# The convolutions' place among the projections, and the normalization behind them moved into their tiles

## The chip, the core and the metric

One core of a Trainium2 chip runs the whole program. The metric is the device time of one execution in microseconds (us). The engines are named as in the profile: PE (TensorE, matrix products; PEld is its weight load), DVE (VectorE), ACT (ScalarE), POOL (GpSimd) and SP (SyncE, which here only issues DMAs). Each works through its own queue in order and waits at semaphores.

## What is computed

One layer of a decoder step: 2048 prompt positions and 32 sample positions share all weights. The input is normalized, multiplied by a wide matrix `w_in`, and split into the inputs of three branches, their SiLU gate paths and three merge gates. The branches are a dilated attention (A), a convolution (B) and a cross-attention into a memory (C).

```python
h = _rmsnorm(x, g_pre) @ w_in
qa, ka, va, za, ub, zb, qc, zc, gt = jnp.split(h, SPLITS, axis=-1)
...
glu = ub[..., :EB] * jax.nn.sigmoid(ub[..., EB:])
conv = causal depthwise convolution of glu, width 31, + conv_b
ob = jax.nn.silu(_layernorm(conv, ln_g, ln_b))
...
mix = (gates[..., 0, :] * ((oa * jax.nn.silu(za)) @ w_pa)
       + gates[..., 1, :] * ((ob * jax.nn.silu(zb)) @ w_pb)
       + gates[..., 2, :] * ((oc * jax.nn.silu(zc)) @ w_pc))
y = x + _rmsnorm(mix @ w_out, g_post)
```

The change concerns branch B: `conv` has 768 channels and 2080 positions, and the LayerNorm runs over the 768 channels of each position.

## The kernel before

All data are float32. A product of two matrices is made from three products of split operands (`gemm`, L160 to L168: high by high, high by low, low by high), so a block of 128 columns of `w_in` against a chunk of positions takes 24 matmuls. A weight block is loaded in one DMA and split by POOL into its high part (L55) and its low part (L56).

**Stages.** `phase_a1` keeps the whole normalized input in SBUF and makes the projections that the branches need: q, k, v (six blocks of 128 columns each), qc (four) and u (six, each of two halves: the gate half, evicted by ACT as a tanh, and the value half, which DVE multiplies into the tile G). In the prediction such a block, or half of a u block, is called a column: there are 32 of them. Each runs over six chunks of positions. A k or v column is also transposed and copied out to rows (`rows_out`, L250 to L265), by PE, DVE and DMA. Two columns of q come first; the others follow in the list `order`: a u block, three others, a u block, three others, and so on. Two DMAs that store a part of the input to memory ride behind each of the first 16 entries.

Behind each u block `conv` (L309 to L352) computes the 31-tap convolution of 128 channels on DVE: the first tap L313, 59 multiply-adds L322 over slices of G into the tile acc, a few small ones for the sample part, and a store of acc to the scratch `d_c` (L335). It also copies the last rows into `so` (L338 to L340), transposes them on PE (L343, L345; PSUM tile trc) and stores them (L350, L351).

Then come, as one stretch, the memory branch (`memory`: `memory_kv` and the cross-attention), the sample attention, the prompt attention, and at the end `phase_c` with the output projections. Beside all of them but the last runs `sweep`: the remaining 40 column blocks of `w_in` (the SiLU paths and gates), whose matmuls write the PSUM tile gg, and whose weights are loaded on ACT's queue.

**conv_norm** (L655 to L687) is the LayerNorm with the SiLU behind it, in nine blocks of 256 positions (the last one of 32) by all six groups of channels. For each: load c (768 KB) from `d_c`; sum the six groups on DVE by one strided reduction (L665); sum over partitions on PE by a matmul with ones (L667); subtract the mean (L668); square on ACT (L671); the same two sums of the squares (L673, L675); variance (L677), square root on ACT and a Newton step on DVE (L63 to L68, from the helper `rsqrt`), multiply (L679); gain and bias on POOL, six instructions (L681); tanh on ACT (L684); the SiLU product on DVE (L685); store (L686). It is a generator: `memory_kv` advances it by one block behind each of its eight weight blocks. Its tiles are its own pool `ln` (c three times, the others once or twice), its PSUM tiles str and sco.

**What sets the order.** The program is written with pools of tiles. A scheduler goes through it once, with a simulated timeline, and fixes each engine's queue. Of the instructions that could start, an engine gets the one with the lowest number, and numbers count up in the order of the text. The helper `later` adds a lag to the numbers of what stands in it:

```python
def later(self, lag):
    p = self.tc.cur_priority
    self.tc.cur_priority = p + lag
    yield
    self.tc.cur_priority = p
```

`conv` is called under `self.later(LAG)` with LAG = 900. Pools are opened and closed like blocks; a pool that is opened later may be laid over the bytes of a closed one. `phase_a1` has psg (four PSUM tiles g), pst (three tr and one trc), cnv (two each of G and GS; one each of gate, acc and others), stg, wr and x12 (the input). With `reuse_waits="tile"`, which psg, pst, cnv and nearly all later pools have, an instruction waits by semaphore only for the users of the bytes that its tile takes.

Of the kernel before, what the change touches and what calls it, by code (L numbers as in the profile page):

```python
# [18 lines left out]
T = S + NS  # L19
# [6 lines left out]
LAG = 900  # L26
# [11 lines left out]
class K:  # L38
# [134 lines left out]
    def phase_a1(self, wp, blocks=None):  # L173
        tc, nc, I, O = self.tc, self.nc, self.I, self.O
        with tc.tile_pool(name="x12", side="right", bufs=1) as xpool, \
                tc.tile_pool(name="stg", side="right", bufs=3) as stg, \
                tc.tile_pool(name="sm1", side="right", bufs=2) as small, \
                tc.tile_pool(name="wr", side="right", bufs=2) as self.wr, \
                tc.tile_pool(name="psg", side="right", bufs=4, space=PSUM, reuse_waits="tile") as psg, \
                tc.tile_pool(name="pst", side="right", bufs=3, space=PSUM, reuse_waits="tile") as pst:  # L180
            for th in (1, 2):
                n = THIRDS[th][1]
                self.X[th] = tuple([xpool.tile([128, n], R32, name=f"x{th}{c}{k}") for k in range(8)]
                                   for c in "hl")
# [12 lines left out]

            with tc.tile_pool(name="cnv", side="right", bufs=1, reuse_waits="tile") as cnv:
                ws.append(self.load_w(wp, self.win(CQ + 128), 8, rp=self.wr))
                for cs, js in [(c, j) for c in (CHUNKS[:1], CHUNKS[1:2], CHUNKS[2:3], CHUNKS[3:4], CHUNKS[4:]) for j in range(2)]:  # L200
                    for s, n in cs:
                        self.chunk("q", js, s, n, ws[js], stg, psg, "g", pst)
                order = []
                rest = [("k", j) for j in range(6)] + [("v", j) for j in range(6)] + \
                       [("q", j) for j in range(2, 6)] + [("qc", j) for j in range(4)]
                for j in range(6):
                    order += [("u", j)] + rest[:3]
                    rest = rest[3:]
                order += rest
                for kind, j in order:  # L210
                    if blocks is not None and (kind, j) not in blocks:
                        continue
                    if kind == "u":
                        gs = self.blk_u(j, wp, stg, cnv, psg, pst)
                        with self.later(LAG):
                            self.conv(j, cnv, pst, *gs)
                    else:
                        self.blk_x(kind, j, wp, stg, psg, pst)
                    for th, c, k in out[:2]:
                        nc.sync.dma_start(self.d_x[th][c][k], self.X[th][c][k].bitcast(F32))  # L220
                    del out[:2]
                assert not out
                self.early = {("za", j): self.load_w(wp, self.win(CZA + 128 * j), 8, rp=self.wr) for j in range(EARLY)}
    def blk_x(self, kind, j, wp, stg, psg, pst):
        w = self.load_w(wp, self.win(self.BASE[kind] + j * 128), 8, rp=self.wr)
# [426 lines left out]
            nc.vector.tensor_add(d, f(O), f(tmp))  # L652


    def conv_norm(self, lp, ps):  # L655
        nc = self.nc
        ones = lp.tile([128, 128], F32, name="ones")
        nc.vector.memset(ones, 1.0)
        W = 256
        for s in range(0, T, W):  # L660
            n = min(W, T - s)
            x = lp.tile([128, 6, W], F32, name="c", bufs=3)[:, :, :n]
            nc.sync.dma_start(x, self.d_c[:, :, s:s + n].rearrange("j p n -> p j n"))
            sm = lp.tile([128, W], F32, name="sm", bufs=2)[:, :n]
            nc.vector.tensor_reduce(sm, x.rearrange("p j n -> p n j"), axis=AX.X, op=ALU.add)  # L665
            p = ps.tile([128, 512], F32, name="str")[:, :n]
            nc.tensor.matmul(p, ones, sm, start=True, stop=True)  # L667
            nc.vector.scalar_tensor_tensor(x, p[:, None, :].to_broadcast([128, 6, n]), -1.0 / EB, x,  # L668
                                           op0=ALU.mult, op1=ALU.add)
            sq = lp.tile([128, 6, W], F32, name="sq", bufs=1)[:, :, :n]  # L670
            nc.scalar.activation(sq, x, AF.Square)  # L671
            sm = lp.tile([128, W], F32, name="sm", bufs=2)[:, :n]
            nc.vector.tensor_reduce(sm, sq.rearrange("p j n -> p n j"), axis=AX.X, op=ALU.add)  # L673
            p = ps.tile([128, 512], F32, name="sco")[:, :n]
            nc.tensor.matmul(p, ones, sm, start=True, stop=True)  # L675
            var = lp.tile([128, W], F32, name="var")[:, :n]
            nc.vector.tensor_scalar(var, p, 1.0 / EB, EPS, op0=ALU.mult, op1=ALU.add)  # L677
            rs = self.rsqrt(lp, var, [128, W], "ln", n)
            nc.vector.tensor_tensor(x, x, rs[:, None, :].to_broadcast([128, 6, n]), op=ALU.mult)  # L679
            for j in range(6):  # L680
                nc.gpsimd.tensor_scalar(x[:, j], x[:, j], self.v("ln_g", j), self.v("ln_b", j),  # L681
                                        op0=ALU.mult, op1=ALU.add)
            t = lp.tile([128, 6, W], F32, name="sq", bufs=1)[:, :, :n]
            nc.scalar.activation(t, x, AF.Tanh, scale=0.5)  # L684
            nc.vector.scalar_tensor_tensor(x, t, 1.0, x, op0=ALU.add, op1=ALU.mult)  # L685
            nc.sync.dma_start(self.d_actb[:, :, s:s + n].rearrange("j p n -> p j n"), x)  # L686
            yield  # L687
# [196 lines left out]
    def memory(self):  # L884
        tc = self.tc
        with tc.tile_pool(name="mem", side="right", bufs=1, reuse_waits="tile") as kp, \
                tc.tile_pool(name="ln", side="right", bufs=1, reuse_waits="tile") as lp, \
                tc.tile_pool(name="lnp", side="right", bufs=1, space=PSUM, reuse_waits="tile") as lps:
            ln = self.conv_norm(lp, lps)
            with tc.tile_pool(name="mem1", side="right", bufs=1, reuse_waits="tile") as mp, \  # L890
                    tc.tile_pool(name="mem1p", side="right", bufs=2, space=PSUM, reuse_waits="tile") as ps, \
                    tc.tile_pool(name="memw", side="right", bufs=2, reuse_waits="tile") as wp:
                KT, VV = self.memory_kv(mp, kp, wp, ps, ln)
            for _ in ln:
                pass
            with tc.tile_pool(name="mem2", side="right", bufs=1, reuse_waits="tile") as mp, \
                    tc.tile_pool(name="mem2p", side="right", bufs=2, space=PSUM, reuse_waits="tile") as ps:
                sc = self.sample_cross(mp, lps)
                for _ in self.cross(mp, ps, KT, VV):
                    for _ in range(3):  # L900
                        next(sc, 0)
                for _ in sc:
                    pass

    def memory_kv(self, mp, kp, wp, ps, ln):
# [12 lines left out]
        rs = self.rsqrt(mp, ss, [128, 2], "mr")  # L918
        for x in range(2):
            nc.vector.tensor_scalar(mts[x], mts[x], rs[:, x:x + 1], None, op0=ALU.mult)  # L920
        for k in range(8):
            t = ps.tile([128, 512], F32, name="tr")
            for x in range(2):
# [3 lines left out]
                                           op0=ALU.mult, op1=ALU.subtract)  # L927
        KT, VV = [], []
        for c in range(8):
            h = c % 4  # L930
            w = self.load_w(wp, I["w_mem_kv"][0, :, 128 * c:128 * c + 128], 8)
            p = ps.tile([128, 512], F32, name="kv")
# [8 lines left out]
            t = ps.tile([128, 512], F32, name="tr")  # L941
# [6 lines left out]
            if c >= 4:  # L948
# [359 lines left out]
```

## Time and profile before

| | |
|---|---|
| median of 3 runs | 3149.05 us (3148.02 to 3153.83) |
| the profiled execution | 3154.4 us, span 3152.6 us |
| PE busy | 3000.2 us, 95% |
| DVE busy | 2014.8 us, 64% |
| ACT, POOL busy | 1124.2 us (36%), 1350.4 us (43%) |
| first tap of the first and last convolution | 154.1 us, 754.9 us |
| last matmul of the projections | 868.3 us |
| blocks of the normalization: first and last Square | 881.9 us, 1125.0 us |
| first and last matmul of the sweep | 869.0 us, 2549.7 us |

The median says what the kernel takes; the stretches and durations are of the one profiled execution. A group's row gives what is written and read, the shape, how often it ran, its busy time, the mean duration in ns, and the idle time of its engine just before it with what ended that. A row of one source line gives the shortest, median and longest duration in ns and the start of the first and of the last. A busy PE is only good as a sign that it has work; idle time of PE is what counts.

### The profile page before, as it was taken

What the parts mean: (1) busy time and instruction counts of PE and PEld (TensorE: products, weight loads), DVE (VectorE), ACT (ScalarE), POOL (GpSimd) and SP (SyncE); (2) the same over time, 40 slices, a digit from 0 to 9 for tenths busy, and PEclk for the clock granted to TensorE, in tenths of its full rate; (3) what the DMA queues carried; (4) which work ended last, traced back from release to release, by engine and by line L of the source; (5) the groups of instructions that cost most, each with busy time, mean ns of one, the idle gap of its engine ahead of it and who ended that gap; (6) DMA issues with size and microseconds to landing.
All of it is one profiled execution on the core that took longest, in us unless ns stands there. A gap on an engine that the chain in (4) does not pass through costs nothing.

```text
span 3152.6 us, 55374 instructions
## 1 busy us (share of the span) xinstructions
PE 3000.2 (95%) x20705; PEld 2839.9 (90%) x20705; DVE 2014.8 (64%) x3734; ACT 1124.2 (36%) x2835; POOL 1350.4 (43%) x1048
## 2 busy tenths in 40 slices
PE   7999999999987999999999999989899979999998
PEld 6899999999987999998999999989898967787897
DVE  5297797796677926465546766666656457556563
ACT  5010010010132433243437575656565523222221
POOL 0121221142356537444256565667676433233240
PEclk9899999999999999999999999999999989999999
DMA  7232222211265454477454656576555487657561
GB/s 250 85 103 80 80 60 61 63 62 50 81 182 167 135 153 144 147 219 239 151 139 116 161 123 163 128 185 150 156 143 152 109 279 227 223 168 227 161 197 53
DMA packets 532218, 454.66 MB, mean 144 GB/s; under 512 B 118191, under 2 KB 458581, under 8 KB 531137
## 3 DMA queue, kind: packets, MB, share of 16 engines
q1 hardware_dynamic: 357502, 335.36, 36.2%
q10 hardware_dynamic: 169840, 105.02, 11.7%
q0 software_dynamic: 4608, 10.75, 1.2%
q8 instruction: 164, 2.69, 0.4%
q14 instruction: 104, 0.85, 0.1%
HBM read 332.96 MB, written 118.04 MB: 143 GB/s over the span
## 4 chain that ended last, share of the span: by engine, by line
PE 70%; DMA 12%; DVE 7%; issue 4%; POOL 3%; ACT 2%; SPq 1%; ACTq 0%; DVEq 0%; POOLq 0%
PE g L166 8%; PE g L167 8%; PE g L168 8%; PE gg L166 6%; PE gg L168 6%; PE gg L167 6%; PE pg L168 3%; PE pg L166 3%; PE pg L167 3%; PE pt L571 2%; DMA cb<-d_cf 2%; PE y L1180 2%; PE y L1179 2%; PE y L1178 2%; PE o L598 1%
## 5 line engine op out<-in xcount | busy, mean ns | idle before, releaser
L166 PE MATMUL gg<-x0h,whi 128*128 128x256 f32 (+1 forms) x2560 | 747.9, 292 | 25.9 <-DVE st L246 12.2
L168 PE MATMUL gg<-x0h,wlo 128*128 128x256 f32 (+1 forms) x2560 | 741.8, 290 | 0.1
L167 PE MATMUL gg<-x0l,whi 128*128 128x256 f32 (+1 forms) x2560 | 741.1, 290 | 0.0
L55 POOL TENSOR_SCALAR whi<-wraw 128x1024 fp32r<-128x1024 f32 x162 | 242.7, 1500 | 928.5 <-PE g L167 524.1
L166 PEld LDWEIGHTS gg<-x0h,whi 128*128 128x128 f32 x2560 | 493.2, 193 | 35.0 <-DVE st L246 13.7
L167 PEld LDWEIGHTS gg<-x0l,whi 128*128 128x128 f32 x2560 | 493.5, 193 | 2.2 <-issue 0.5
L168 PEld LDWEIGHTS gg<-x0h,wlo 128*128 128x128 f32 x2560 | 493.2, 193 | 2.2 <-POOL wlo L56 0.3
L322 DVE SCALAR_TENSOR_TENSOR acc<-G,cw,acc 128x1536 f32<-128x1536 f32 (+15 forms) x354 | 480.8, 1408 | 0.3
L56 POOL TENSOR_TENSOR wlo<-wraw,whi 128x1024 fp32r<-128x1024 f32 x162 | 417.0, 2575 | 9.4 <-PE gg L168 0.2
L155 POOL TENSOR_TENSOR clo<-craw,chi 128x768 fp32r<-128x768 f32 (+1 forms) x96 | 174.1, 1815 | 346.0 <-ACT chi L154 329.8
L627 ACT ACTIVATE P<-T,stm 128x128 f32<-128x128 f32 (+1 forms) x576 | 260.8, 455 | 141.0 <-DVE stm L625 94.8
L239 ACT ACTIVATE st<-g 128x384 f32<-128x384 f32 (+1 forms) x132 | 60.2, 461 | 570.7 <-PE g L168 550.7
L166 PE MATMUL pg<-ac,chi 128*128 128x512 f32 (+1 forms) x640 | 229.4, 359 | 16.6 <-ACT chi L154 8.7
L625 DVE CUSTOM_DVE_ANT_0 T<-s,bias 128x128 f32<-128x128 f32 (+1 forms) x576 | 191.5, 357 | 80.8 <-PE s L617 47.0
L167 PE MATMUL pg<-ac,chi 128*128 128x512 f32 (+1 forms) x640 | 228.8, 358 | 6.3 <-DVE ac L1198 6.3
L168 PE MATMUL pg<-ac,clo 128*128 128x512 f32 (+1 forms) x640 | 227.6, 357 | 3.6 <-POOL clo L155 3.6
L576 DVE TENSOR_TENSOR pl<-pt,ph 128x512 fp32r<-128x512 f32 x240 | 155.6, 652 | 52.4 <-ACT ph L575 48.9
L168 PE MATMUL g<-x0h,wlo 128*128 128x384 f32 x544 | 184.3, 339 | 2.9 <-POOL wlo L56 2.9
L166 PE MATMUL g<-x0h,whi 128*128 128x384 f32 x544 | 183.6, 338 | 2.6 <-ACT st L239 2.3
L167 PE MATMUL g<-x1l,whi 128*128 128x384 f32 x544 | 186.0, 342 | 0.0
L167 PE MATMUL g<-x0l,whi 128*128 128x384 f32 x544 | 185.8, 342 | 0.0
L168 PE MATMUL g<-x1h,wlo 128*128 128x384 f32 x544 | 185.8, 342 | 0.0
(330 smaller groups left out, 7425.0 us busy)
## 6 DMA issues: line engine op xcount, KB each, us to landing
wraw<-in_w_in ACTq DMA_DIRECT2D x119, 512.0 KB
d_g<-st ACTq DMA_DIRECT2D x168, 128.0 KB
cb<-d_cf SPq DMA_DIRECT2D x72, 256.0 KB
g<-d_g SPq DMA_DIRECT2D x72, 256.0 KB
wraw<-in_w_in SPq DMA_DIRECT2D x35, 512.0 KB
kvc<-in_cache_k_win SPq DMA_DIRECT2D x8, 1536.0 KB
kvc<-in_cache_v_win SPq DMA_DIRECT2D x8, 1536.0 KB
raw<-d_q SPq DMA_DIRECT2D x48, 256.0 KB
```

What stands on the lines that cost most here:

```text
L55: nc.gpsimd.tensor_scalar(hi, raw, 1.0, 1.0, op0=ALU.mult, op1=ALU.mult)
L56: nc.gpsimd.tensor_sub(lo, raw, hi.bitcast(F32))
L155: nc.gpsimd.tensor_sub(lo, raw, hi.bitcast(F32))
L166: nc.tensor.matmul(ps, hi[:, k, :], h, start=k == 0, stop=False)
L167: nc.tensor.matmul(ps, hi[:, k, :], l, start=False, stop=False)
L168: nc.tensor.matmul(ps, lo[:, k, :], h, start=False, stop=k == kb - 1)
L322: nc.vector.scalar_tensor_tensor(a3[:, lo:hi], G[:, src:src + hi - lo, 2 - m:130 - m], w, a3[:, lo:hi], op0=ALU.mult, op1=ALU.add)
L571: nc.tensor.transpose(t[:, 128 * x:128 * x + 128], pc, self.ident)
L576: nc.vector.tensor_tensor(pl[:, :w], t[:, :w], ph[:, :w].bitcast(F32), op=ALU.subtract)
L625: nc.vector.tensor_tensor_reduce(sc[:, :w], t[:, o:o + w], bias[:, 256 - w:256], 1.0, 3.0e38, ALU.add, ALU.min, m)
L627: nc.scalar.activation(P[:, o:o + w], sc[:, :w], AF.Exp, bias=m, scale=-1.0, accum_out=self.stl[:, col:col + 1])
L1178: nc.tensor.matmul(y[:m, c, :], ah[:, ts_], bh[:, cs], start=k == 0, stop=False)
```

## The change

Three things. The list `order` puts two other columns behind each u block instead of three; so eight columns (q2 to q5 and the four of qc) stand behind the last u block's two. The normalization is traced in `phase_a1`: its generator gets `cnv` and `pst`, one block is traced behind each of those eight last columns, under `later(LAG)`, and the ninth behind them all. It takes the convolutions' tiles for its own: x is a G, the sum a GS, squares and tanh are `gate`, the rows of the variance and its root a piece of `acc`, and both PSUM sums are `tr`. And its sums over the six groups are made by additions: five of 256 positions for the first, one of 768 and two of 256 for the second. The pool `ln` goes, and `memory_kv` no longer advances the generator.

```diff
                 for j in range(6):
-                    order += [("u", j)] + rest[:3]
-                    rest = rest[3:]
+                    order += [("u", j)] + rest[:2]
+                    rest = rest[2:]
                 order += rest
+                ln = self.conv_norm(cnv, pst)
                 for kind, j in order:
...
+                    if (kind, j) in rest:
+                        with self.later(LAG):
+                            next(ln, 0)
                 assert not out
+                for _ in ln:
+                    pass
...
-    def conv_norm(self, lp, ps):
+    def conv_norm(self, cnv, ps):
...
+            x = six(cnv.tile([128, 16, 130], F32, name="G", bufs=2).rearrange("p r i -> p (r i)"))
             nc.sync.dma_start(x, self.d_c[:, :, s:s + n].rearrange("j p n -> p j n"))
-            sm = lp.tile([128, W], F32, name="sm", bufs=2)[:, :n]
-            nc.vector.tensor_reduce(sm, x.rearrange("p j n -> p n j"), axis=AX.X, op=ALU.add)
-            p = ps.tile([128, 512], F32, name="str")[:, :n]
+            sm = cnv.tile([128, 8, 34], F32, name="GS", bufs=2).rearrange("p b w -> p (b w)")[:, :n]
+            nc.vector.tensor_add(sm, x[:, 0], x[:, 1])
+            for j in range(2, 6):
+                nc.vector.tensor_add(sm, sm, x[:, j])
+            p = ps.tile([128, 512], F32, name="tr")[:, :n]
             nc.tensor.matmul(p, ones, sm, start=True, stop=True)
...
-            sq = lp.tile([128, 6, W], F32, name="sq", bufs=1)[:, :, :n]
+            sq = six(cnv.tile([128, T], F32, name="gate"))
             nc.scalar.activation(sq, x, AF.Square)
-            sm = lp.tile([128, W], F32, name="sm", bufs=2)[:, :n]
-            nc.vector.tensor_reduce(sm, sq.rearrange("p j n -> p n j"), axis=AX.X, op=ALU.add)
-            p = ps.tile([128, 512], F32, name="sco")[:, :n]
-            nc.tensor.matmul(p, ones, sm, start=True, stop=True)
-            var = lp.tile([128, W], F32, name="var")[:, :n]
+            nc.vector.tensor_add(sq[:, 0:3], sq[:, 0:3], sq[:, 3:6])
+            nc.vector.tensor_add(sq[:, 0], sq[:, 0], sq[:, 1])
+            nc.vector.tensor_add(sq[:, 0], sq[:, 0], sq[:, 2])
+            p = ps.tile([128, 512], F32, name="tr")[:, :n]
+            nc.tensor.matmul(p, ones, sq[:, 0], start=True, stop=True)
+            rows = cnv.tile([128, T], F32, name="acc")
+            var, sd, r = row(0), row(1), row(2)
...
-            t = lp.tile([128, 6, W], F32, name="sq", bufs=1)[:, :, :n]
+            t = six(cnv.tile([128, T], F32, name="gate"))
...
     def memory(self):
-                tc.tile_pool(name="ln", side="right", bufs=1, reuse_waits="tile") as lp, \
...
-                KT, VV = self.memory_kv(mp, kp, wp, ps, ln)
-            for _ in ln:
-                pass
+                KT, VV = self.memory_kv(mp, kp, wp, ps)
...
-            next(ln, 0)
         return KT, VV
```

More of the change, by code (lines that the diff above doesn't have):

```diff
@@ L652, in o_out @@
             nc.vector.tensor_add(d, f(O), f(tmp))
-    def conv_norm(self, lp, ps):
+    def conv_norm(self, cnv, ps):
         nc = self.nc
-        ones = lp.tile([128, 128], F32, name="ones")
+        ones = cnv.tile([128, 128], F32, name="ones")
         nc.vector.memset(ones, 1.0)
@@ L661, in conv_norm, with six, row @@
             n = min(W, T - s)
-            x = lp.tile([128, 6, W], F32, name="c", bufs=3)[:, :, :n]
-            nc.sync.dma_start(x, self.d_c[:, :, s:s + n].rearrange("j p n -> p j n"))
-            sm = lp.tile([128, W], F32, name="sm", bufs=2)[:, :n]
-            nc.vector.tensor_reduce(sm, x.rearrange("p j n -> p n j"), axis=AX.X, op=ALU.add)
-            p = ps.tile([128, 512], F32, name="str")[:, :n]
+            def six(t):
+                return t[:, :6 * n].rearrange("p (j n) -> p j n", j=6)
+            def row(o):
+                return rows[:, o * n:o * n + n]
+            x = six(cnv.tile([128, 16, 130], F32, name="G", bufs=2).rearrange("p r i -> p (r i)"))
+            nc.sync.dma_start(x, self.d_c[:, :, s:s + n].rearrange("j p n -> p j n"))
+            sm = cnv.tile([128, 8, 34], F32, name="GS", bufs=2).rearrange("p b w -> p (b w)")[:, :n]
[3 more added lines that the diff above has]
+            p = ps.tile([128, 512], F32, name="tr")[:, :n]
             nc.tensor.matmul(p, ones, sm, start=True, stop=True)
@@ L886, in memory @@
         with tc.tile_pool(name="mem", side="right", bufs=1, reuse_waits="tile") as kp, \
-                tc.tile_pool(name="ln", side="right", bufs=1, reuse_waits="tile") as lp, \
                 tc.tile_pool(name="lnp", side="right", bufs=1, space=PSUM, reuse_waits="tile") as lps:
-            ln = self.conv_norm(lp, lps)
             with tc.tile_pool(name="mem1", side="right", bufs=1, reuse_waits="tile") as mp, \
@@ L903, in memory, with memory_kv @@
                     pass
-    def memory_kv(self, mp, kp, wp, ps, ln):
+    def memory_kv(self, mp, kp, wp, ps):
         nc, I, O = self.nc, self.I, self.O
```

9 lines of the change are left out of this document (7 added, 2 removed).

## The prediction

> **What bounds the kernel now.** I read the stages first (from a time, to a time, length, then busy time and instruction count of PE, its weight loads, DVE, ACT and POOL, the granted clock, DMA share, GB/s):
>
> ```profile
> 154.00:755.00 601.00, 595.79 (x3829) 592.87 (x3828) 483.84 (x510) 55.27 (x120) 145.96 (x55) 1.00 0.23 71
> 755.00:868.00 113.00, 113.00 (x716) 112.91 (x716) 84.57 (x78) 13.44 (x29) 42.64 (x10) 1.00 0.22 72
> 868.00:1140.00 272.00, 235.24 (x1815) 226.93 (x1814) 208.29 (x276) 99.82 (x185) 155.64 (x142) 0.95 0.53 163
> 1140.00:2550.00 1410.00, 1358.56 (x10873) 1322.53 (x10872) 826.00 (x2242) 739.51 (x2142) 814.51 (x733) 0.98 0.58 156
> 2550.00:3152.60 602.60, 567.44 (x2737) 469.12 (x2736) 353.07 (x507) 162.03 (x250) 173.84 (x95) 0.97 0.60 189
> ```
> TensorE is the bound. In the projections (154 to 868) it idles 5.2 us; in 868 to 1140, where the normalization runs beside the memory branch, 36.8; after that 3.6% until the sweep's last matmul (2549.7, next row), behind which the final stage starts. The sweep (gates and SiLU paths) is PE's filler, so each microsecond that PE idles between 154 and 2550 is paid at the end, and only PE's idle time counts. DVE, 80% busy in the convolutions, costs nothing by itself.
>
> ```profile
> L168 PE MATMUL gg<-x0h,wlo x2560: 274/283/775, 869.0 to 2549.7; 128*128 128x256 f32 x173, 128*128 128x288 f32 x24
> ```
>
> **The order of the columns.** A "column" is one 128-wide block of a projection.
>
> ```profile
> L313 DVE TENSOR_SCALAR acc<-G,cw,vecs x6: 1519/1521/1522, 154.1 to 754.9; 128x2048 f32<-128x2048 f32 x6
> ```
> ```profile
> L168 PE MATMUL g<-x2h,wlo x544: 274/292/415, 65.2 to 868.3; 128*128 128x256 f32 x92, 128*128 128x288 f32 x90
> ```
> Behind the last u block stand five columns, 113.4 us or 22.7 each. A convolution starts every 120.2 us, so a k or v column, with its transposes, takes (120.2 - 2 x 22.7) / 3 = 24.9. The reorder moves no work off PE: 32 columns still end at 868. But u5 ends five columns earlier, near 630, its convolution (84.5 us from 754.9 to its last store's issue, L322 below) near 715 to 740, and eight q and qc columns (181.6 us) stand last. DVE has 483.84 x 120.2 / 601 = 96.8 us of work per old period, about 3 less in the new one of 95.2, so it just keeps up: 0 as the value, up to 10 of stall as the end.
>
> **When PE does the sums.** The norm's instructions are traced under `later(900)`: their place in PE's order is 900 instructions behind. The convolution's three small transposes are traced the same way and show what that means on a PE that is never idle:
>
> ```profile
> L340 DVE TENSOR_SCALAR so<-GS x6: 266/268/272, 158.7 to 784.9; 128x240 f32<-128x240 f32 x6
> ```
> ```profile
> L343 PE MATMUL trc<-ident,so x6: 270/271/272, 284.9 to 868.5; 128*30 128x128 f32 x6
> ```
> The first one's input was ready at 159.0 and PE did it at 284.9. By the code its number is 975 behind u0's end; three k columns (192 instructions each with two stores of x) and u1 (315) use up 891, and 84/192 of a column is left: 154.1 + 74.7 + 45.4 + 10.9 = 285.1. So a low number is simply not served before its turn.
>
> A q column is 159 instructions (a load, two splits, 144 matmuls, six evictions, six stores). The norm's first matmul is its seventh or eighth instruction: (900 + 7) / 159 = 5.7 columns or 129.4 us after the column behind which it is traced. Block 0 stands behind q2, which ends at 868.3 - 7 x 22.7 = 709.4, so PE gets to it at 838.8, although its data are there by about 755 (conv 5, a store and a load); block 1 at 861.5; block 2 would be 884, behind the last column. Two of nine blocks run beside projections, seven do not.
>
> **What waits for the other seven.** The old norm had tiles and PSUM banks of its own. Now it holds `cnv` (G, gate, acc) and the `tr` banks of `pst`. The next stage's pools are laid over these: I take the PSUM pools of the sweep and of the memory branch, opened when psg and pst close, to stand on their banks, and in the program before, the sweep's weight buffers lie over G and the memory branch's first over acc. Does a new pool wait for its own bytes alone, or for the old pool's last user? Before:
>
> ```profile
> L322 DVE SCALAR_TENSOR_TENSOR acc<-G,cw,acc x354: 332/1397/4262, 158.9 to 837.3; 128x1792 f32<-128x1792 f32 x12, 128x1664 f32<-128x1664 f32 x12, 128x1536 f32<-128x1536 f32 x12, 128x1408 f32<-128x1408 f32 x12
> ```
> ```profile
> L351 SPq DMA_DIRECT2D out_conv_s<-sr x6: 364/369/408, 290.5 to 872.2; - x6
> ```
> ```profile
> 878.89 1.90 ACTq L150 DMA_DIRECT2D wraw<-in_w_in  x2
> ```
> ```profile
> 880.76 1.31 SPq L150 DMA_DIRECT2D wraw<-in_w_mem_kv  x2
> ```
> G and acc were last used at 839, yet the sweep's and the memory branch's first weight loads, on two queues, are issued only at 879 and 881, just after `cnv`'s last user, the store of 872.2, can have landed. That reads as waiting for the pool's last user. And tr banks are handed out as they come free, so none is safe for another pool while sums are to come. So sweep and memory matmuls wait for the norm's end, and PE has the sums alone.
>
> **How long the norm takes.** Rows of the old one (869 to 1133):
>
> ```profile
> L681 POOL TENSOR_SCALAR c<-c,vecs 128x256 f32<-128x256 f32 x48 | 26.4, 564 | 10.6 <-DVE sl L1005 5.4 <-DVE c L679 5.2
> L673 DVE TENSOR_REDUCE sm<-sq 128x256 f32<-128x1536 f32 x8 | 23.0, 2876 | 9.5 <-ACT sq L671 9.5
> L665 DVE TENSOR_REDUCE sm<-c 128x256 f32<-128x1536 f32 x8 | 22.7, 2840 | 0.7 <-DMA c<-d_c 0.7
> ...
> L679 DVE TENSOR_TENSOR c<-c,lnr 128x1536 f32<-128x1536 f32 x8 | 14.0, 1753 | 0.1
> L64 DVE RECIPROCAL lnr<-lns 128x256 f32<-128x256 f32 x8 | 13.9, 1743 | 4.0 <-ACT lns L63 4.0
> L668 DVE SCALAR_TENSOR_TENSOR c<-str,c 128x1536 f32<-128x1536 f32 x8 | 13.9, 1736 | 1.2 <-PE str L667 1.2
> ...
> L684 ACT ACTIVATE sq<-c 128x1536 f32<-128x1536 f32 x8 | 11.9, 1487 | 9.3 <-POOL c L681 9.3
> L671 ACT ACTIVATE sq<-c 128x1536 f32<-128x1536 f32 x8 | 11.9, 1485 | 21.7 <-DVE c L685 21.7
> ...
> L675 PE MATMUL sco<-sm,ones 128*128 128x256 f32 x16 | 6.7, 510 | 14.9 <-DVE sm L673 14.9
> L667 PE MATMUL str<-sm,ones 128*128 128x256 f32 x16 | 6.5, 492 | 6.1 <-DVE sm L665 4.5 <-DVE mss L917 1.5
> ...
> L68 DVE TENSOR_TENSOR lnr<-lns,lnr 128x256 f32<-128x256 f32 x8 | 3.4, 421 | 0.1
> L63 ACT ACTIVATE lns<-var 128x256 f32<-128x256 f32 x8 | 3.3, 418 | 0.5 <-DMA sb<-d_exs 0.5
> L677 DVE TENSOR_SCALAR var<-sco 128x256 f32<-128x256 f32 x8 | 3.3, 415 | 0.0
> ```
> ```profile
> L685 DVE SCALAR_TENSOR_TENSOR c<-sq,c x9: 359/2439/12593, 908.9 to 1132.5; 128x1536 f32<-128x1536 f32 x8, 128x192 f32<-128x192 f32 x1
> ```
> The Square of a block waited for the previous block's L685 (21.7 of idle time): one buffer holds both the squares and the tanh, and it goes round in order. `gate` is again one buffer, so a block's period is its chain from Square to L685. The second sum becomes one addition of 768 (about 0.95, between L68's 0.42 for 256 and L679's 1.75 for 1536) and two of 256: 1.8 for 2.9. The first becomes five, 2.1 for 2.8, but is off this chain. Chain: 1.49 + 1.8 + 1.0 (two matmuls) + 0.42 + 0.42 + 1.74 + 4 x 0.4 (the Newton step, nearest L68) + 1.75 + 6 x 0.56 + 1.49 + 2.44 = 17.5, and about ten handovers of 0.1: 18.5. Ends: 16.8 (no handovers, L685 as short as L679), and 30.4, the old mean spacing (243 us for eight), which had the memory branch in between. I take 18.5, since the wait above keeps that branch out.
>
> The nine loads and nine stores ride on SP's queue behind 0.4 us issues, POOL's gains (3.4 a block) behind splits with a column of lead, sqrt and tanh tables on an idle ACT (13.44 of 113 us): nothing, as long as conv 5 is in time; a load waiting on SP would hold the q stores behind it, and PE after three `st` and four `g` buffers.
>
> Block 1's Square: 861.5 + 1.0 + 1.74 = 864.2. Block 8's, seven periods on: 993.7; its short second sum is read near 996. So PE is without columns, sweep and memory for 996 - 868 = 128 us. The norm's own matmuls there (seven blocks x 4 x 0.5, 13) were PE work before too: **+115**.
>
> **What is gained.** In the memory branch PE no longer waits for sums, 14.9 + 4.5, and less for DVE's gate products:
>
> ```profile
> PE gg L166 <- DVE st L246: 10.1, 9, 1.8
> ```
> I take half of this: **-24** (19 to 30).
>
> **POOL's splits.** A weight split was held while DVE ran unbroken multiply-adds:
>
> ```profile
> 657.08 21.74 POOL L55 TENSOR_SCALAR whi<-wraw 128x1024 fp32r<-128x1024 f32 x1 [18.76 <-PE g L167]
> ```
> ```profile
> 823.00 17.29 POOL L55 TENSOR_SCALAR whi<-wraw 128x1024 fp32r<-128x1024 f32 x1 [17.00 <-PE g L167]
> ```
> Such holds cost the 5.2 us in conv 4 and 5; a split has a column (22.7) of lead. Now only conv 5's second half runs beside q columns: a hold of up to 42 (half of 84.5), so 0 to 23 of stall; I take the old 5 again, net **0** (-5 to +18). The Trainium skill (SBUF — State Buffer, "Who interferes with whom") says that a VectorE instruction with two SBUF inputs and a GpSimd one that reads SBUF block each other until the first finishes. By that a hold ends with one multiply-add, this term would be -5 and the median 3235; the trace does not agree, 21.74 spans some twenty of them.
>
> **Sum:** 115 - 24 + 0 = +91, so 3154.4 becomes 3245 for a profiled execution, and the median 3149 becomes **3240**. Its own range: periods of 16.8, the best relief and no stall give 115 - 12 - 30 - 5 = +68; a period of 20, relief 19 and 23 of stall 115 + 10 - 19 + 18 = +124: 3215 to 3275.
>
> **Rivals.** *Sums held back, but nothing waits for the norm:* seven blocks run beside the memory branch as before; two of nine leave it (-5): 3144. For it: the sweep's first matmul at 869 waited for nothing. Against: the loads at 879. *PE takes sums as they come, the next stage waits:* first Square near 750, ninth 148 later at 898, an overhang of 32 less 4 of sums, less 24, and up to 15 more if conv 5 slips: about 3160. Against: 284.9. *Faster: sums served at once and no wait for the pools.* DVE idles 28 us of the last 113 even with conv 5 in them; the place is the eight q columns, the price the 24, hence 3125; it decides if the first sum is on PE before about 770, not 839. This is what the Trainium skill (Perfetto Trace Analysis, "Optimization Strategy") would have one expect, that interleaving stages with different bounds may help; the row of 284.9 speaks against it here.
>
> **Numbers.** Main 0.72, second rival 0.09, first 0.12, faster one 0.07. 3155 to 3290 leaves out the first and the last and a little of the top. A measurement tells about 0.2% (6.3 us) from no change: faster 0.11 (the last and a third of the first), same 0.08, slower 0.81.
>
> **What would show it.** PE's first matmul of the norm near 839 and its second block near 861; Squares 18 to 19 us apart after 868; a PE nearly idle from 868 to about 990, and the first `gg` matmul there instead of at 869; no DVE sums in the memory branch. Wrong it is if `gg` starts at 869, or if sums are on PE by 770.

## The result, and the profile after

The changed kernel takes 3246.48 us (median of four runs; three lie between 3240.75 and 3247.33, the fourth was disturbed, took 10297.06 and is left out of the ratio) against 3148.53 for the kernel before in the same comparison: a ratio of 1.0302, 95% interval 1.0268 to 1.0336. The profiled execution took 3240.75 us, span 3238.8, against 3154.4 and 3152.6 before. So 86.2 us of span are to be explained.

First the end of the columns and the sweep, as rows of a source line in the profile after (shortest, median and longest duration in ns, start of the first and of the last):

```profile
L168 PE MATMUL g<-x2h,wlo x544: 274/292/469, 67.4 to 864.3; 128*128 128x256 f32 x92, 128*128 128x288 f32 x90
L168 PE MATMUL gg<-x0h,wlo x2560: 274/283/580, 1015.4 to 2648.0; 128*128 128x256 f32 x173, 128*128 128x288 f32 x24
```

The columns' last matmul starts at 864.3 instead of 868.3, but the sweep starts at 1015 instead of 869. The normalization's first sums on PE, its Squares and the convolutions' transposes:

```profile
L682 PE MATMUL tr<-GS,ones x18: 377/632/795, 834.9 to 1002.2; 128*128 128x256 f32 x16, 128*128 128x32 f32 x2
L686 ACT ACTIVATE gate<-G x9: 362/1482/1487, 837.3 to 1011.9; 128x1536 f32<-128x1536 f32 x8, 128x192 f32<-128x192 f32 x1
L349 PE MATMUL trc<-ident,so x6: 270/270/272, 283.5 to 768.1; 128*30 128x128 f32 x6
```

The nine Squares start at 837.3, 861.5, 888.3, 911.8, 934.1, 953.7, 973.3, 993.2 and 1011.9. What PE waited for between the columns' end and the sweep's start (engine, line, waited for: us, times, longest):

```profile
PE tr L691 <- DVE gate L689: 81.2, 7, 17.4
PE tr L682 <- DVE GS L680: 50.5, 7, 10.5
```

So PE did little there but wait for the next sum, 131.7 us in 14 waits. The stretches of the profile after (from, to, length, busy time and count of PE, of its weight loads, of DVE, ACT, POOL, granted clock, DMA share, GB/s): the gap, the sweep, the final stage.

```profile
864.30:1014.70 150.40, 17.34 (x36) 8.04 (x35) 90.34 (x141) 44.93 (x43) 31.65 (x46) 0.51 0.31 95
1014.70:2648.00 1633.30, 1571.38 (x12641) 1534.94 (x12639) 904.36 (x2411) 789.89 (x2278) 938.41 (x823) 0.98 0.56 154
2648.00:3238.80 590.80, 563.42 (x2738) 465.38 (x2737) 346.29 (x502) 161.59 (x250) 168.59 (x93) 0.98 0.60 187
```

and the sweep's stretch before, to set beside the second row (the final stage before, 602.60, stands in the prediction):

```profile
868.60:2550.00 1681.40, 1593.20 (x12682) 1548.90 (x12680) 1033.75 (x2516) 839.33 (x2327) 970.15 (x874) 0.98 0.57 157
```

The account: columns 864.3 - 868.6 = -4.3 (868.6 is the end of the last matmul, 864.3 the start of its counterpart, so 0.3 of this belongs to the gap); a gap of +150.4; the sweep 1633.3 - 1681.4 = -48.1, of which 21.8 is less busy time of PE (the sums that left, and more; see below) and 26.3 is less idle time (61.9 for 88.2); the final stage 590.8 - 602.6 = -11.8. Together +86.2.

### The profile page after: what moved, and what is told of

The parts are those of the page before. It is cut to its first block, busy times and chain, and to the rows that moved or that the text cites. A ratio compares the mean times of both kernels' runs of the same rounds, so it can differ in the third digit from the quotient of the medians.

```text
span 3238.8 us, 55544 instructions
## 1 busy us (share of the span) xinstructions
PE 2990.8 (92%) x20705; PEld 2829.2 (87%) x20705; DVE 1971.2 (61%) x3788; ACT 1126.5 (35%) x2835; POOL 1358.1 (42%) x1048
## 4 chain that ended last, share of the span: by engine, by line
PE 55%; DMA 6%; DVE 3%; issue 2%; POOL 2%; ACT 1%; SPq 0%; ACTq 0%; DVEq 0%; POOLq 0%
PE gg L166 8%; PE gg L168 8%; PE gg L167 8%; PE pg L168 3%; PE pg L167 3%; PE pg L166 3%; PE pt L577 3%; PE y L1197 2%; PE y L1196 2%; PE y L1195 2%; PE o L604 2%; PE s L622 2%; PE s L623 2%; PE o L603 2%; PE tr L884 1%
## 5 line engine op out<-in xcount | busy, mean ns | idle before, releaser
L166 PE MATMUL gg<-x0h,whi 128*128 128x256 f32 (+1 forms) x2560 | 743.7, 291 | 18.1 <-DMA x0h<-d_x 7.3
L55 POOL TENSOR_SCALAR whi<-wraw 128x1024 fp32r<-128x1024 f32 x162 | 251.7, 1554 | 924.6 <-PE g L167 540.3
L166 PEld LDWEIGHTS gg<-x0h,whi 128*128 128x128 f32 x2560 | 491.3, 192 | 23.8 <-ACT st L249 7.6
L166 PE MATMUL pg<-ac,chi 128*128 128x512 f32 (+1 forms) x640 | 226.7, 356 | 12.4 <-ACT chi L154 6.1
L166 PE MATMUL g<-x0h,whi 128*128 128x384 f32 x544 | 183.0, 337 | 1.7 <-ACT st L245 1.2
L166 PE MATMUL g<-x1h,whi 128*128 128x384 f32 x544 | 182.7, 340 | 0.3 <-ACT x1h L135 0.3
```

Of the source, the lines that this page charges most:

```text
L55: nc.gpsimd.tensor_scalar(hi, raw, 1.0, 1.0, op0=ALU.mult, op1=ALU.mult)
L166: nc.tensor.matmul(ps, hi[:, k, :], h, start=k == 0, stop=False)
```

## The experiments

Theory: PE's place for a sum is 900 numbers behind, so seven of nine blocks come after the columns; and the next stage's pools wait for the last user of the pools below, so PE has nothing else meanwhile. The ratios are to the kernel before, run beside each.

**The reorder alone** (order_only):

```diff
-                    order += [("u", j)] + rest[:3]
-                    rest = rest[3:]
+                    order += [("u", j)] + rest[:2]
+                    rest = rest[2:]
```

> The kernel before with one line changed: two other columns behind each u block instead of three; the normalization stays in the memory branch, in its own tiles, with its reductions. Theory (the reorder costs about nothing, the loss comes from the normalization in phase_a1): the last projection matmul ends at 864 to 872, the convolutions' first taps are about 96 us apart, the normalization's Squares stay near 30 us apart from about 880 on, the first gg at about 869, and the time is 3149 with -10 to +18. Rival (the denser u phase starves PE through DVE and the weight splits, and this is a large part of the loss): PE idles 20 us or more before 868 and the time is 3180 or more.

3153.23 us, ratio 1.0019 (1.0006 to 1.0033). The columns end at 862, PE idles 1.3 us from 154 to there, the sweep starts at 862. The loss is not in the reorder.

**The additions alone** (adds_only: in the kernel before; the first sum likewise by five additions):

```diff
-            nc.vector.tensor_reduce(sm, sq.rearrange("p j n -> p n j"), axis=AX.X, op=ALU.add)
+            nc.vector.tensor_add(sq[:, 0:3], sq[:, 0:3], sq[:, 3:6])
+            nc.vector.tensor_add(sq[:, 0], sq[:, 0], sq[:, 1])
+            nc.vector.tensor_add(sm, sq[:, 0], sq[:, 2])
```

> The kernel before with one thing changed: the normalization's sums over the six groups by additions (five of 256 positions; one of 768 and two of 256) instead of the two strided reductions; order, place and tiles as before. Theory (PE waits there for sums; a first sum is 0.7 us shorter and a second 1.1): PE's idle time in 868 to 1140 falls from 36.8 by at most 9 times 1.8, time 3150 less 0 to 16, most likely 3145. Rival (nothing, other waits take their place): within 0.2% of 3150.

3162.89 us, ratio 1.0031 (1.0015 to 1.0046): neither. DVE's rows from 868 to 1140, first the reductions in the kernel before, then the additions:

```profile
L673 DVE TENSOR_REDUCE sm<-sq 128x256 f32<-128x1536 f32 (+1 forms) x9 | 23.5, 2613 | 9.9 <-ACT sq L671 9.9
L665 DVE TENSOR_REDUCE sm<-c 128x256 f32<-128x1536 f32 (+1 forms) x9 | 23.2, 2577 | 0.7 <-DMA c<-d_c 0.7
```
```profile
L667 DVE TENSOR_TENSOR sm<-sm,c 128x256 f32<-128x256 f32 (+1 forms) x36 | 19.7, 547 | 0.8
L675 DVE TENSOR_TENSOR sq<-sq 128x768 f32<-128x768 f32 (+1 forms) x9 | 10.8, 1196 | 9.5 <-ACT sq L673 9.5
L677 DVE TENSOR_TENSOR sm<-sq 128x256 f32<-128x256 f32 (+1 forms) x9 | 5.6, 624 | 0.2
L676 DVE TENSOR_TENSOR sq<-sq 128x256 f32<-128x256 f32 (+1 forms) x9 | 4.2, 472 | 0.1
L665 DVE TENSOR_TENSOR sm<-c 128x256 f32<-128x256 f32 (+1 forms) x9 | 3.5, 393 | 1.0 <-DMA c<-d_c 1.0
```

The additions of the first sum took 23.2 us in all, no less than the reductions, and those of the second 20.6 for 23.5; the expectation had 0.7 and 1.1 us less for each. PE's waits for the two sums fall from 19.4 to 5.1 us in 868 to 1140, but PE waits 18.6 instead of 10.1 for the gate products (st) of DVE, and the sweep's last matmul comes 8 us later. What the waits for sums lost, others took.

**Which wait holds the sweep** (trc: the sums in the one tile trc, bank 3, of the same pool):

```diff
-            p = ps.tile([128, 512], F32, name="tr")[:, :n]
+            p = ps.tile([128, 512], F32, name="trc", bufs=1)[:, :n]
```

> The changed kernel with the normalization's sums in the tile trc (bank 3) instead of tr (banks 0 to 2); both belong to the pool pst. The sweep's gg has banks 0 and 1, which the normalization then never touches. Theory (a new pool waits for the last user of the old pool that it is laid over, not for its own bytes): first gg at 1010 to 1030 as in the changed kernel, time within 12 us of 3246. Rival (a pool waits for its own bytes alone): first gg at about 866, beside the normalization, at least the early weight block's 72 matmuls (15 us) come ahead, time 3231 or less.

3245.35 us, ratio 1.0310 (1.0293 to 1.0326). The sweep, in trc:

```profile
L168 PE MATMUL gg<-x0h,wlo x2560: 274/283/582, 1017.6 to 2649.9; 128*128 128x256 f32 x173, 128*128 128x288 f32 x24
```

gg stands on banks 0 and 1, which the normalization no longer touches here, and still starts at 1017 (its first matmul, L166, at 1017.0). It comes behind the pool's last user, though its bytes are free.

**The sums in another pool's bank** (own_bank), and its control (three_g, only the first of these lines):

```diff
-                tc.tile_pool(name="psg", side="right", bufs=4, space=PSUM, reuse_waits="tile") as psg, \
+                tc.tile_pool(name="psg", side="right", bufs=3, space=PSUM, reuse_waits="tile") as psg, \
-                ln = self.conv_norm(cnv, pst)
+                ln = self.conv_norm(cnv, psg)
-            p = ps.tile([128, 512], F32, name="tr")[:, :n]
+            p = ps.tile([128, 512], F32, name="sn", bufs=1)[:, :n]
```

> The changed kernel with the sums in a PSUM tile of their own, sn, in bank 7, taken from the pool psg, where g has three tiles instead of four. Theory (a pool waits for the old pool's last user): the sweep's pool stands on pst's banks and no longer waits, so gg starts at about 866, but only with two chunks (48 matmuls, 10 us), until its st tiles, which lie over cnv, are wanted; the memory branch's PSUM pool stands on pst's and psg's banks and waits still, though none of its four banks holds a sum: its first transposes (L942) only at 1000 to 1020; time about 3236 (3222 to 3250). Rival (own bytes alone): the memory branch's transposes at about 880, its products fill PE, time 3130 to 3190.

> The changed kernel with three g tiles instead of four in the projections and nothing else (the sums stay in tr; the pool pst moves up by one bank, and bank 0 stays free): a control for own_bank and own_pool, which came out slower than the changed kernel by 9 and 17 us where 10 less and 71 less were expected. Theory (three g tiles make the projections longer, columns' end at 871 to 873 instead of 864.6, and this is the loss of own_bank): 3253 (3250 to 3260). Rival (three g tiles cost nothing): 3246 within 4, columns' end at 866 or before; the loss of own_bank is then elsewhere.

own_bank: 3255.13 us, ratio 1.0342 (1.0322 to 1.0363). three_g: 3263.27 us, 1.0380 (1.0361 to 1.0399). The sweep and the memory branch's transposes in own_bank:

```profile
L168 PE MATMUL gg<-x0h,wlo x2560: 274/283/562, 871.5 to 2663.9; 128*128 128x256 f32 x173, 128*128 128x288 f32 x24
L942 PE MATMUL tr<-ident,mt x16: 270/418/475, 1022.5 to 1031.1; 128*128 128x128 f32 x16
```

Both places come out as the pool theory has them: with pst free of sums the sweep starts at once, and stops after 48 matmuls, as expected, until 1033, behind the normalization's end; the memory branch, whose PSUM pool reaches over psg too, waits to 1022. The time was off because three g tiles cost 0.8% by themselves (columns' end at 872.5, and more later than these runs explain); against that control own_bank gains 8 us (12 by the ratios), for 10 expected.

**A pool of their own for the sums** (own_pool; psg with three g as above):

```diff
+                tc.tile_pool(name="psn", side="right", bufs=1, space=PSUM, reuse_waits="tile") as psn, \
-                ln = self.conv_norm(cnv, pst)
+                ln = self.conv_norm(cnv, psn)
```

> The changed kernel, still under later(900), with the sums in a PSUM pool of their own (one bank; g has three tiles instead of four). No pool of the memory branch stands on that bank. Theory (the old pool's last user is what holds the next stage): the memory branch and the cross-attention, some 215 us of PE's work, now run beside the normalization, its transposes by 890 at the latest; the sweep still stops after 48 matmuls, since its st and weight tiles lie over cnv, until the normalization's end, which comes later than 1014 since the sums are again served in turn with the memory branch's matmuls. PE's idle time falls from 133 us to 30 to 90: time 3246 plus 7 (three g tiles, as in own_bank) less 45 to 105, about 3175 (3145 to 3210). Rival (the whole next stage waits for cnv, or for the sums by its numbers): first transposes of the memory branch at 1000 or later, time 3240 or more.

3263.83 us, ratio 1.0348 (1.0331 to 1.0365): the mechanism came, the time did not. The transposes are at 894, the sweep stops until the normalization is done, and that is now at 1066:

```profile
L943 PE MATMUL tr<-ident,mt x16: 271/416/477, 894.1 to 905.5; 128*128 128x128 f32 x16
L1047 PE MATMUL str<-ident,xk x64: 272/273/475, 1066.5 to 1132.6; 128*128 128x128 f32 x64
```

One premise of the expectation was wrong: in the program as built the sample part of the memory branch has its PSUM tile str on the bank of sn. Its input was loaded from 965 on, but its first matmul (L1047) starts at 1066.5, released by L695, which reads the last sum. 400 us from the columns' end, in own_pool and then in the changed kernel:

```profile
873.00:1066.00 193.00, 99.68 (x501) 84.53 (x499) 144.10 (x247) 69.81 (x118) 83.48 (x92) 0.70 0.38 116
1066.00:1273.00 207.00, 198.22 (x1545) 189.25 (x1545) 99.23 (x249) 63.64 (x177) 103.18 (x91) 0.98 0.44 133
```
```profile
864.00:1015.00 151.00, 17.94 (x40) 8.64 (x39) 90.87 (x143) 45.17 (x44) 31.65 (x46) 0.51 0.31 95
1015.00:1264.00 249.00, 248.65 (x2009) 242.22 (x2009) 132.65 (x323) 87.28 (x247) 150.19 (x132) 0.99 0.47 141
```

Count the matmuls, not the busy time: 2046 against 2049. PE got 461 more matmuls done beside the normalization (48 of them the sweep's, the others nearly all the memory branch's), but DVE had 144 us of work there instead of 91, and the normalization ended 51 us later (8.5 of it because the columns ended later), and after it the sweep had more to catch up. The expectation took PE's durations as its work: they overlap. 99.68 us of busy time are 501 matmuls, at the 0.124 us each of the last row only 62 us.

**Sums at once** (lag0):

```diff
-                        with self.later(LAG):
+                        with self.later(0):
                             next(ln, 0)
```

> The changed kernel with the normalization's eight blocks traced under later(0) instead of later(900), so that PE takes a sum once it is ready. Theory (the hold in PE's order makes seven of nine blocks late): first Square at 740 to 760 instead of 837, Squares 18.5 to 23 us apart beside the columns, three blocks left behind the columns' end, first gg at 900 to 925 instead of 1014.7, time 3246 less 90 to 115: about 3143 (3125 to 3165). Rival (not the hold, but DVE or the one buffer gate beside the columns paces the blocks): Squares 28 us or more apart, first gg at 960 or later, time 3195 or more.

3171.89 us, ratio 1.0080 (1.0061 to 1.0099). The Squares and the sweep:

```profile
L686 ACT ACTIVATE gate<-G x9: 363/1487/1494, 750.3 to 949.0; 128x1536 f32<-128x1536 f32 x8, 128x192 f32<-128x192 f32 x1
L166 PE MATMUL gg<-x0h,whi x2560: 274/283/588, 952.0 to 2587.9; 128*128 128x256 f32 x173, 128*128 128x288 f32 x24
```

First Square at 750.3, the next five 25.6 apart; columns' end at 888.9, sweep's start at 952. To lift the hold alone brings back 75 of the 98 us, the largest part; the expected value was 29 too fast, since a block beside columns takes 25.6 and the columns themselves end 24 later (from 154 on PE idles 12.2 us and is busy 722.7, for 1.2 and 709.1 in the changed kernel).

**Two tiles for squares and tanh** (two_buf, still with the lag; lag0_two without it). The variance's rows move to prod and st_in:

```diff
-            sq = six(cnv.tile([128, T], F32, name="gate"))
+            sq = six(cnv.tile([128, T], F32, name="acc"))
```

> The changed kernel, still under later(900), with the squares in acc and the tanh in gate, so that a block's Square no longer waits for the block before (the rows of the variance move to prod and st_in, one copy less). Theory (the stretch without other work is seven periods of the chain through the one tile gate): the period is then set by DVE's own work on a block (13.3 us) or by G's two tiles (load, chain, store over two blocks: about 15): Squares 14 to 16.5 apart after block 1 instead of 21.5 on average, first gg at 970 to 985 instead of 1014.7, time about 3209 (3198 to 3222). Rival (loads, stores and handovers set the period, not gate): Squares 19 or more apart, time 3232 or more.

> Both together: sums at once (later(0)) and the two tiles for squares and tanh; sums still in tr. Without the two tiles the Squares were 25.5 apart beside the columns and gg began at 952. Theory: with two tiles 18 to 21 apart beside the columns (a load waits on SP's queue behind stores of q, POOL's splits and gains share that engine), so about two blocks are left at the columns' end near 888, first gg at 900 to 920, time 3172 less 32 to 52: 3130 (3118 to 3142), faster than before. Rival (beside the columns SP's queue and DVE's order pace the blocks at one per column, 25 us, whatever the buffers): first gg at 930 or later, time 3150 or more.

two_buf: 3231.27 us, ratio 1.0240 (1.0221 to 1.0260); sweep's start 994.5, Squares 18.7 apart behind block 1 instead of 21.5. So gate cost about 3 us a block on the average, but only 1 where the pace is even (18.4 to 18.6 between the last full blocks, for 19.6); the spacing and the time are nearly the rival's, whose loads, stores and handovers set the pace. That it is the round through G's two tiles (load, chain, store) was not tried by itself. lag0_two: 3158.77 us, ratio 1.0023 (1.0009 to 1.0036); Squares 20.6 apart on the average, as the theory had it, sweep's start 922.9, between theory and rival, the time the rival's.

**All of it** (lag0_two_pool: lag0_two with own_pool's psn; lag0_pool: without the two tiles; red_two_pool: lag0_two_pool with the two reductions back).

> The changed kernel with sums at once (later(0)) and in a PSUM pool of their own, but with the one tile gate for squares and tanh. Theory (the sums' own pool lets the memory branch start at the columns' end, but matmuls on a half-idle PE run slowly, as in own_pool): first transposes of the memory branch by 910, normalization's end at 960 to 975, time 3172 less 15 to 35: 3147 (3135 to 3160). Rival (the own pool gives only what the two tiles gave already): as lag0, 3165 or more.

> lag0_two with the sums in a PSUM pool of their own (three g tiles). Theory (what is left of the loss is PE's idle time between the columns' end and the normalization's): the memory branch fills it, its transposes come within 15 us of the columns' end, idle time of PE up to the first 100 us behind the columns below 30; three g tiles cost up to 7; time 3120 (3105 to 3138), the fastest of all. Rival (nothing left to hide): same as lag0_two within 6 us, or slower by the three g tiles.

> lag0_two_pool, the fastest so far, with the two strided reductions back in place of the additions. Theory (beside the last columns a block's chain counts, and the additions shorten it by 0.7 to 1.1 us a sum: 40.0 us of DVE's time in all for the additions in lag0_two_pool, 46.7 for the reductions in the kernel before): the last Square comes 3 to 12 us later than 915, time 3137 plus 0 to 12, most likely 3142. Rival (as in adds_only, where the additions came out slower by 0.3%): time 3137 less 5 to 12.

lag0_pool: 3191.16 us, 1.0133 (1.0112 to 1.0153), slower than lag0, which neither side had. lag0_two_pool: 3137.32 us, ratio 0.9954 (0.9936 to 0.9971), at the slow end of its range. red_two_pool: 3134.01 us, ratio 0.9946 (0.9926 to 0.9966), between its two expectations and not to be told from lag0_two_pool. The last two beat both kernels. The stretches of lag0_two_pool:

```profile
154.00:888.20 734.20, 722.64 (x4577) 716.64 (x4576) 651.42 (x708) 106.40 (x182) 218.82 (x100) 0.99 0.27 84
888.20:2537.60 1649.40, 1581.39 (x12651) 1542.84 (x12649) 925.15 (x2453) 800.99 (x2294) 955.04 (x839) 0.98 0.56 155
2537.60:3129.10 591.50, 562.45 (x2736) 464.53 (x2736) 351.50 (x502) 161.60 (x250) 170.83 (x93) 0.99 0.60 187
```

The columns end 19.6 us later than before (6.4 us more idle time, 13 us more busy time with the sums between them), the gap is gone (the sweep starts at the columns' end, the memory branch's transposes at 905), and sweep and final stage are 32.0 and 11.1 shorter than before. The additions bring nothing here either.

## Why the prediction was right, and where it was not

**What bounds.** PE's idle time up to the sweep's end was paid at the end: a gap of 150.4, less the 48.1 by which the sweep got shorter and the 4.3 of the columns, moved the sweep's last matmul by 98.

**The order of the columns.** The columns ended at 864.3 for 868, and conv 5 was done in time: a block's load was issued at 733. POOL's splits cost nothing, and of the 5.2 us of idle time before 1.2 were left (1.3 in order_only). The term taken as 0 was -4. The longest split of the profile after took 20.43 us (702 to 722), beside 17 multiply-adds of conv 5. The Trainium skill (SBUF — State Buffer, "Who interferes with whom") says that whoever issues first gets the shared ports for the whole instruction and the other blocks; that a hold would then end with one multiply-add was again not seen.

**When PE does the sums.** Forecast 838.8 and 861.5 for the first two blocks, found 834.9 and 858.4. lag0 shows that it is the lag.

**What waits.** Forecast from two load issues, shown by trc and own_bank: a pool comes behind the last user of the old pool under any of its banks. In the programs built from these two kernels the matmuls in question (the first gg of trc, the first L942 of own_bank) carry no semaphore for the sums; they stand behind the last sum in PE's queue. So it is the order fixed by the scheduler that waits for the pool's last user, and that a semaphore waits only for a tile's own bytes stays true beside it.

**How long the norm takes.** Here a step failed in size. The seven periods from block 1's Square to block 8's were 26.8, 23.5, 22.3, 19.6, 19.6, 19.9 and 18.7 us, for 18.5, so the gap was 150 us for 128. The failed sentence is the one that puts the loads, the stores and POOL's gains at "nothing". In the first period block 1's gains (L703), ready at 876.9, stood behind splits of the memory branch's weights and took 4.2 us where 3.2 is usual, together some 4 us:

```profile
875.34 3.72 POOL L56 TENSOR_TENSOR wlo<-wraw,whi 128x1024 fp32r<-128x1024 f32 x1
879.04 1.04 POOL L55 TENSOR_SCALAR whi<-wraw 128x1024 fp32r<-128x1024 f32 x1
880.07 4.19 POOL L703 TENSOR_SCALAR G<-G,vecs 128x256 f32<-128x256 f32 x6
```

In the second it was a load. Block 3's load and what stood behind it, in the profile after:

```profile
890.24 0.45 SPq L708 DMA_DIRECT2D d_actb<-G  x1
893.98 1.75 DVE L696 RECIPROCAL acc<-acc 128x256 f32<-128x256 f32 x1 [0.48 <-ACT acc L695]
895.27 0.45 SPq L676 DMA_DIRECT2D G<-d_c  x1
900.01 0.42 DVE L678 TENSOR_TENSOR GS<-G 128x256 f32<-128x256 f32 x1 [4.28 <-DMA G<-d_c]
900.83 0.42 DVE L697 TENSOR_TENSOR acc<-acc 128x256 f32<-128x256 f32 x1
```

The load (L676) needs block 1's G, whose store (L708) could go at 888.3 and was issued at 890.24, behind a weight load and DMAs of the sample attention on SP's queue, issued at 0.4 and 0.7 us each; store and load took 9.8 us. DVE's queue has block 3's first addition (L678) ahead of block 2's Newton step (L697), which had its input at 895.7. So block 2 stood for 5 us behind another block's load. All such waits in the gap (us, times, longest):

```profile
DVE GS L678 <- DMA G<-d_c: 11.0, 7, 4.3
```

So the waits for loads are about half of the 22 us that were missing; the rest lies with the gains of block 1, with a copy of the sample attention (L732) that waited 3.1 us for its DMA in block 3's way, and with the next block's additions, which DVE does between the steps of a block, though the forecast had them off the chain. How much each is worth was not tried by itself.

**What is gained.** Forecast -24, found -26.3 of idle time in the sweep, -4.3 in the columns and -11.8 in the final stage, where nothing was expected. The 13 us subtracted for the sums were right. Their rows before, from 868.6 to 2550:

```profile
L675 PE MATMUL sco<-sm,ones 128*128 128x256 f32 (+1 forms) x18 | 7.0, 479 | 14.9 <-DVE sm L673 14.9
L667 PE MATMUL str<-sm,ones 128*128 128x256 f32 (+1 forms) x18 | 6.8, 463 | 6.1 <-DVE sm L665 4.5 <-DVE mss L917 1.5
```

These are 13.8 of the 21.8 us of busy time that left the sweep. The other 8.0 are a gain that was not forecast: the same matmuls were recorded shorter, those of gg 2221.4 us in all for 2230.8. Terms of +115 and -24 were really 150.4 - 13.8 = +136.6 and -50.4. The forecast of 3240 is so near 3246 because a loss that was too small by 22 and a gain that was too small by 26 nearly cancel; the mechanism and its places were right, the exactness was luck.

**The rivals.** "PE takes sums as they come" was priced 3160; lag0 took 3172. Its overhang was 63 us, not 32, so the price was nearer than its working. "Nothing waits for the norm" was priced 3144: own_pool shows that to lift the PSUM wait alone is not this case (the sweep's st tiles and weights lie over cnv) and that what then runs beside the norm slows it. The faster rival came only with three changes together, and is then 0.5% faster and not 0.8% (the second tile and the own pool with the lag kept were not run together). That interleaving stages with different bounds may help, as the Trainium skill (Perfetto Trace Analysis, "Optimization Strategy") says, came true here only in the two kernels where the held sums, the shared pool and the one tile are all gone.

**Open.** Why the final stage is shorter in every kernel whose normalization has left the memory branch (602.6 us before, 606 to 607 in order_only and adds_only, 598 in red_two_pool, 588 to 594 in the others); in the changed kernel its PE idles 27 us instead of 35, and waits 3.3 us instead of 12.4 for DVE's ac and mix; why DVE is sooner there is not known. Why three g tiles cost 0.8% in three_g, when in lag0_two_pool the columns end only 2 us later than in lag0_two. And why lag0_pool is 0.5% slower than lag0: by 1100 us PE had done about as many matmuls behind the columns in both (1219 and 1206), so the loss comes later.

## What to carry to other kernels

Work that is to run beside another stage needs three things: a place in the bottleneck engine's order when its data are ready (a lag that suits one use can hold another), no pool in common with what comes after, and buffers enough that its loads, stores and chain don't follow one another. Before hiding work in a closed stage's tiles, ask which pool opens next on the same bytes or banks: a pool may be ordered behind the last user of the whole old pool. And price PE's work by the count of matmuls at their interval, never by the sum of their durations.

## What the runs showed of the hardware

A PE with gaps is slower while it works, too. The same matmuls of the memory branch in own_pool, between 894 and 957 with gaps, and in the changed kernel beside the sweep (count, busy us, mean ns, idle before them):

```profile
L167 PE MATMUL kv<-ml,whi 128*128 128x256 f32 x64 | 22.2, 349 | 0.0
```
```profile
L167 PE MATMUL kv<-ml,whi 128*128 128x256 f32 x64 | 18.0, 286 | 0.0
```

349 ns against 286, at a granted clock of 0.76 from 894 to 957 (0.70 in the whole stretch, row above) against 0.99. Ends of matmuls are modelled, but the starts say the same: in own_pool they are 0.21 us apart at 898 and 0.12 at 903. The Trainium skill (TensorE: Matmul & The Clock Gate, "Part 1: The HAM clock gate") says that idle windows halve the clock until PE has been busy for a while; these rows agree, and 0.51 is the granted clock of the changed kernel's gap.

DVE and POOL slow each other both ways. In lag0 one addition of 256 positions, median 0.42 us, lay beside a split:

```profile
790.02 2.42 POOL L56 TENSOR_TENSOR wlo<-wraw,whi 128x1024 fp32r<-128x1024 f32 x1
```
```profile
790.13 2.59 DVE L680 TENSOR_TENSOR GS<-GS,G 128x256 f32<-128x256 f32 x1
```

It took 2.59 us, as long as the split; the other way round, a split (L55) that takes 1.05 us alone took the 20.43 above. Stretched additions are in adds_only too: the longest of 256 positions took 2.49 us, and all together were hardly shorter than the reductions. That POOL's splits are what stretched them there was not tried by itself.
